# A hybrid attention and DeltaNet layer on one core: two-tensor work off GpSimd in the attention stage, eight buffers for the reloaded attention branch, three DeltaNet tiles in places of their own

## The chip, the core and the metric

The kernel runs on one core of a Trainium2 chip, in one launch. The metric is the device time of that launch in microseconds. Engines are named as in the profile: PE is TensorE, DVE is VectorE, ACT is ScalarE, POOL is GpSimd, and SP issues most of the DMAs. Three runs of the kernel before took 1337.43, 1338.98 and 1342.21 us; the median is 1338.98 us.

## What is computed

One step of a one-layer encoder over 592 tokens (16 meta tokens, 512 of the prompt, 64 of a sample) of width 1024. The parts that matter here:

```
h = RMSNorm(x);  proj = h @ w_in        # columns: q, k, v | DeltaNet q, k, v | z | beta, alpha | gates A, B
A: 8 heads, two 64-wide softmax maps per head, RMS norm of each q and k map (q_norm, k_norm),
   relative bias, block-causal mask, w = p0 - lam * p1, o = w @ v, RMS norm per head
B: 8 heads of 128, causal conv + SiLU, gated delta rule;  o_b = RMSNorm(o_b) * gdn_norm * SiLU(z)
mix = sigmoid(gA) * (o_a @ w_br_a) + sigmoid(gB) * (o_b @ w_br_b);  x = x + mix @ w_out
x = x + relu(RMSNorm(x) @ w_up)^2 @ w_down
```

The outputs are the new rows, and the keys, values and states of both streams.

## The kernel before, in words

Every weight product is taken in three passes of a reduced-precision float type: a matrix is split into a high part (ACT, a cast) and a low part (a subtraction), and high*high, high*low and low*high are summed in PSUM. The weights are streamed in tasks of 256 columns (`stream`, line 300): SP loads two halves of 512 KB, ACT casts them to `wh`, and `lower` (line 348) subtracts to `wl`, on DVE or POOL as `VG` (line 287) decides. `feat` (line 470) runs one task: four groups of 24 matmuls (8 chunks of the contraction, 3 passes each), each group into one of three PSUM banks `pg`.

The order of the whole program is written at build time. `drive` (line 449) lets the weight tasks go forward by 8 matmuls at a time, and between them advances side chains (DeltaNet, attention units, norms) when a model of the engines' times (`Pace`, line 53) says that their inputs are ready. Each engine then runs its own list in that order, and so does each DMA queue. `VG` compares the model's times of DVE and POOL; the model knows no mutual hindrance of the two.

The tasks run in this order: DeltaNet q, k and v, z (SiLU gate), attention q, k, v of the first four heads, gate B, q, k, v of the other four, gate A, branch B (`bb`), branch A (`ba`), w_out, up and down.

- `delta(g)` (line 881), once for each half of the DeltaNet heads: at its end it scales the output, transposes it into `pf`, ACT multiplies it by `gdn_norm`, and SP stores it to `ob_d`. The second half loads its v only after the first half is done.
- `attn_tasks` (line 1199) evacuate q, k, v with an ACT copy and store them to `at_d`. `attend_prep` (line 1233) reloads one head and does three POOL multiplications of 128x640: k and q by their inverse norms `rn`, and k by `k_norm` (`kn_bc`).
- `attend` (line 1291) has 40 units (8 heads of 5 query blocks): scores on PE, bias and maximum on DVE, exponentials on ACT, the combination of the two maps on DVE, transposes on PE, values on PE.
- `load_ob` (line 1418) runs beside them. It reloads the DeltaNet output (`ma`) and z (`mb`), multiplies them on POOL, and waits for `hidden`, which is set when gate A, the last user of the normed input `hh`, `hl`, has issued its matmuls. Then it splits the eight chunks into the memory of `hh` and `hl`, and the branch B tasks start (`br_b_tasks`, line 1437). Three of the four may run beside the attention (HELD, line 47).
- After the attention's memory is released, `load_oa` (line 1481) reloads the attention output through SP in two buffers and splits it for branch A. `residual` (line 1489) loads x again through POOL's queue, one buffer, and transposes it.

The lines that set the places are 589 to 600, 1682 and 1692:

```
ob = [x[:, :, 0:TQ] for x in (hh, hl)]
ab_ = Tags(pace, at_, qk=4, v=3, past=3, sc=SC, mx=6, wT=WT, ob=8, oz=2, ...
mg = Tags(pace, mg_, oa=2, xt=1)
```

Of the kernel before, what the change touches and what calls it, by code (L numbers as in the profile page):

```python
# [8 lines left out]
F32 = mybir.dt.float32  # L9
# [8 lines left out]
P = 128  # L18
# [27 lines left out]
WT = 2  # L46
HELD = 3
MASKED = -32768.0

# [161 lines left out]
def stream_step_kernel(  # L211
# [30 lines left out]
    def bank(name):  # L242
        return pt.tile([P, 512], F32, name=name, tag="pt")
# [36 lines left out]
    def store(dst, src):  # L280
        pace.store(Q, dst, src)
# [5 lines left out]
    def VG(out, n):  # L287

        if "tail" in done:
            return V  # L290
        return V if max(pace.t["DVE"], pace.t["PE"]) + 1.05 * n <= max(pace.t["POOL"], pace.t["PE"]) + out * n else G
# [177 lines left out]

    def feat(xh, xl, nm, evac, m=P, ms=(0, P), halves=QHALVES, after="start", last=None, turn=False):  # L470

        def body(w):
            parts, full = [(h, c) for h in range(len(ms)) for c in (halves[::-1] if turn and h else halves)], deque()
            if "start" not in done:
                parts.sort(key=lambda x: x[1])
            for h, (a, b) in parts:
                while len(full) == PG:
                    yield False
                ps = pg.tile([P, 512], F32, name=f"pg_{nm}{h}{a}", tag="pg")
                n = 0  # L480
                for kc in range(KC):
                    for ww, xx in ((w[0], xh), (w[0], xl), (w[1], xh)):
                        xk = xx[kc] if isinstance(xx, list) else xx[:, kc]
                        TE.matmul(ps[:m, :b - a], ww[:, kc, ms[h]:ms[h] + m], xk[:, a:b], start=n == 0, stop=n == 3 * KC - 1)
                        n += 1
                        if n % QUANTUM == 0 and n < 3 * KC:
                            yield
                full.append((h, ps[:m, :b - a], a, b))
                if last and h == len(ms) - 1 and b == TQ:
                    done.add(last[0])  # L490
                    while last[1] not in done:
                        yield False
                while full and after in done:
                    evac(*full.popleft())
                yield
        return body
# [91 lines left out]
    at_d = [dp.tile([H, P, NT, P], F32, name=f"at_d{i}") for i in range(3)]  # L588
    z_d, oa_d, mb_d = ([dp.tile([P, TQ], F32, name=f"{nm}{j}") for j in range(KC)] for nm in ("z_d", "oa_d", "mb_d"))
    ob_d = dp.tile([H, P, T], F32, name="ob_d")  # L590
# [8 lines left out]
    hq, lq = (x[:, :, N0:T] for x in (hh, hl))  # L599
    ob = [x[:, :, 0:TQ] for x in (hh, hl)]  # L600

# [279 lines left out]
    def delta(g):  # L881
# [251 lines left out]
        V.scalar_tensor_tensor(c1, c1, 0.5, r, ALU.mult, ALU.mult)  # L1133
        yield
        for s in range(NT + 1):
            if s:
                c0, n = TILES[s - 1]
                pf = bank(f"pf{g}{s}").rearrange("p (h i) -> p h i", h=4)
# [4 lines left out]
                store(ob_d[h0:h0 + 4, :, c0:c0 + n].rearrange("h d i -> d h i"), oT[:, :, :n])  # L1143
# [35 lines left out]
    def z_tasks(cs):  # L1179
        out = []  # L1180
        for c in cs:
            def evac(h, ps, a, b, c=c):
# [7 lines left out]
                if b == TQ:  # L1190
                    store(z_d[j], th)
                    done.add(f"z{c}")
            out.append(Task(f"z{c}", w_in[0], OFF_Z + c * 256, feat(hq, lq, f"z{c}", evac)))
# [39 lines left out]
    def attend_prep(hd):  # L1233
# [184 lines left out]
    def load_ob():  # L1418

        while not has("delta0", "delta1", *[f"z{c}" for c in range(4)])():  # L1420
# [12 lines left out]
        for j in range(KC):  # L1433
            split(ob[0][:, j], ob[1][:, j], obs[j])
        done.add("ob")

    def br_b_tasks():
        out = []
        for c in range(4):
# [10 lines left out]
            def body(w, c=c, evac=evac):  # L1450
                yield from feat(ob[0], ob[1], f"bb{c}", evac)(w)
                if c == 3:
                    done.add("br_b")
# [27 lines left out]
    def load_oa():  # L1481
        for j in range(KC):
            a = mg.tile([P, TQ], F32, name=f"oa{j}", tag="oa")
            Q.dma_start(a, oa_d[j])
            yield
            split(late["oh"][j], late["ol"][j], a)
        done.add("oa")

    def residual():

        x1 = late["x1"]
        for t, (c0, n) in enumerate(QTILES):
            xt = mg.tile([P, D], F32, name=f"x_r{t}", tag="xt")
            G.dma_start(xt[:n], x_prompt[0, c0:c0 + n] if t < 4 else x_sample[0])
            yield pace.free(xt) + 4000
            for q in range(2):
# [177 lines left out]
    with pool("delta", side="right") as db_:  # L1674
# [4 lines left out]
        chains.append(Chain(conv_out()))  # L1679
        drive(lambda: not chains and has("delta0", "delta1")())  # L1680
    with pool("attn", side="right") as at_:
        ab_ = Tags(pace, at_, qk=4, v=3, past=3, sc=SC, mx=6, wT=WT, ob=8, oz=2, aoss=3, bias=2, osb=3,
                   aqT0=2, aqT1=2, akT0=2, akT1=2)
# [4 lines left out]
    with pool("mix", side="right") as mp:  # L1688
        for nm in ("mxh", "mxl"):
            late[nm] = [mp.tile([P, TQ], F32R, name=f"{nm}{j}", tag=f"{nm}{j}") for j in range(KC)]  # L1690
        with pool("merge", side="right") as mg_:
            mg = Tags(pace, mg_, oa=2, xt=1)
            for nm in ("oh", "ol"):
                late[nm] = [mg.tile([P, TQ], F32R, name=f"{nm}{j}", tag=f"{nm}{j}") for j in range(KC)]
            done.add("merge")
            chains.append(Chain(load_oa()))
            drive(has("br_b"))
            hp_cm.__exit__(None, None, None)
            xp = ctx.enter_context(pool("x1"))
# [66 lines left out]
```

## Time and profile before

| | us |
|---|---|
| median of three runs | 1338.98 |
| the profiled execution, its own time | 1335.53 |
| its span, first to last instruction | 1333.6 |
| PE busy in the span | 1286.3 |
| DVE, ACT, POOL busy | 855.6, 611.3, 181.4 |

The span is in 25,734 instructions. A row of a group gives engine, operation, what is written from what, the shape and the count, then the busy time and the mean duration of one, then the idle time ahead of it and what ended that. Most rows carry the line of a helper that issues every operation, so they are told apart by the names of tiles. Consecutive matmuls overlap, so the duration of one is more than twice the step from one to the next. The attention's units run from about 584 to 784 us of the span, branch A starts at about 818 us.

### The profile page before, as it was taken

The page shows a single profiled execution, that of the slowest core. Times are in us where ns is not written, and L with a number is a line of the kernel's source. Part 1 is how long each engine was busy: PE and PEld are TensorE (multiplying, and loading weights), DVE is VectorE, ACT ScalarE, POOL GpSimd, SP SyncE. Part 2 cuts the span into 40 slices and gives each one's busy share as a digit, 9 for nine tenths or more (in the row PEclk, how much of TensorE's full clock was granted, in tenths as well). Part 3 has the DMA queues.
Part 4 walks back from the last instruction along what each step waited for, and adds up shares of the span by engine and source line. Part 5 has one row for each costly group of instructions (what it writes and reads, how often), then busy time and mean ns, then how long its engine had stood idle before and what let it go on. Part 6 is the DMA issues. An engine that isn't in the chain of part 4 may idle for free.

```text
span 1333.6 us, 25734 instructions
## 1 busy us (share of the span) xinstructions
PE 1286.3 (96%) x10177; PEld 1242.1 (93%) x10177; DVE 855.6 (64%) x1842; ACT 611.3 (46%) x1438; POOL 181.4 (14%) x251
## 2 busy tenths in 40 slices
PE   7999999999999999999798997999999999999998
PEld 5989999999999999998787886999999999999998
DVE  5766999334377525267777853345678678678687
ACT  5565544333752333366465742224453443453442
POOL 3111513100330000252422102310000000000000
PEclk9999999999999999999899898999999999999999
DMA  6324244423644423774444336542223322323322
GB/s 165 91 67 155 61 145 129 144 81 88 206 118 135 144 60 95 228 235 129 161 131 142 122 124 211 182 141 80 80 80 95 96 80 87 105 62 97 110 76 76
DMA packets 163806, 160.55 MB, mean 120 GB/s; under 512 B 23531, under 2 KB 143613, under 8 KB 163686
## 3 DMA queue, kind: packets, MB, share of 16 engines
q1 hardware_dynamic: 161574, 153.11, 37.7%
q0 software_dynamic: 2112, 5.80, 1.5%
q8 instruction: 80, 1.31, 0.4%
q14 instruction: 40, 0.33, 0.1%
HBM read 123.94 MB, written 37.88 MB: 121 GB/s over the span
## 4 chain that ended last, share of the span: by engine, by line
PE 83%; DVE 6%; DMA 4%; ACT 3%; issue 2%; SPq 0%; POOL 0%; DVEq 0%; ACTq 0%; POOLq 0%
PE pg_u L165 15%; PE pg_a L165 11%; PE pg_d L165 8%; PE pg_g L165 7%; PE pg_ba L165 4%; PE pg_z L165 4%; PE pg_o L165 4%; PE pd_dn L165 4%; PE pa_dn L165 4%; PE pc_dn L165 4%; PE pg_bb L165 3%; PE ppo L165 2%; PE pb_dn L165 2%; DMA bias_d<-bv_d 2%; PE po L165 1%
## 5 line engine op out<-in xcount | busy, mean ns | idle before, releaser
L165 PE MATMUL pg_u<-h2h,wh_u 128*128 128x288 f32 x512 | 151.5, 296 | 0.0
L165 PE MATMUL pg_u<-h2h,wl_u 128*128 128x288 f32 x512 | 151.3, 296 | 0.0
L165 PE MATMUL pg_u<-h2l,wh_u 128*128 128x288 f32 x512 | 151.3, 295 | 0.0
L165 PE MATMUL pg_a<-wh_a,hh 128*128 128x256 f32 (+1 forms) x480 | 136.3, 284 | 1.3 <-ACT sq L165 1.3
L165 PE MATMUL pg_a<-wh_a,hl 128*128 128x256 f32 (+1 forms) x480 | 136.3, 284 | 0.0
L165 PE MATMUL pg_a<-wl_a,hh 128*128 128x256 f32 (+1 forms) x480 | 135.4, 282 | 0.0
L165 PE MATMUL pg_d<-hh,wh_d 128*128 128x336 f32 (+1 forms) x384 | 115.8, 302 | 0.0
L165 PE MATMUL pg_d<-hl,wh_d 128*128 128x336 f32 (+1 forms) x384 | 115.6, 301 | 0.0
L165 PE MATMUL pg_d<-hh,wl_d 128*128 128x336 f32 (+1 forms) x384 | 115.5, 301 | 0.0
L165 PEld LDWEIGHTS pg_u<-h2h,wh_u 128*128 128x128 f32 x512 | 96.1, 188 | 0.1
L165 PEld LDWEIGHTS pg_u<-h2l,wh_u 128*128 128x128 f32 x512 | 96.1, 188 | 0.0
L165 PEld LDWEIGHTS pg_u<-h2h,wl_u 128*128 128x128 f32 x512 | 96.1, 188 | 0.0
L165 PEld LDWEIGHTS pg_a<-wh_a,hh 128*128 128x128 f32 (+1 forms) x480 | 86.5, 180 | 2.4 <-ACT sq L165 1.9
L165 PEld LDWEIGHTS pg_a<-wh_a,hl 128*128 128x128 f32 (+1 forms) x480 | 86.6, 180 | 0.7 <-issue 0.6
L165 PEld LDWEIGHTS pg_a<-wl_a,hh 128*128 128x128 f32 (+1 forms) x480 | 86.5, 180 | 0.4 <-issue 0.2
L165 PE MATMUL pg_g<-hh,wl_g 128*128 128x288 f32 x256 | 78.2, 305 | 0.0
L165 PE MATMUL pg_g<-hh,wh_g 128*128 128x288 f32 x256 | 77.8, 304 | 0.0
L165 PE MATMUL pg_g<-hl,wh_g 128*128 128x288 f32 x256 | 77.7, 303 | 0.0
L165 PEld LDWEIGHTS pg_d<-hh,wl_d 128*128 128x128 f32 x384 | 72.9, 190 | 0.7 <-issue 0.6
L165 PEld LDWEIGHTS pg_d<-hl,wh_d 128*128 128x128 f32 x384 | 72.6, 189 | 1.0 <-issue 0.6
L165 PEld LDWEIGHTS pg_d<-hh,wh_d 128*128 128x128 f32 x384 | 72.7, 189 | 0.2
L165 DVE SCALAR_TENSOR_TENSOR cv_d<-pre_d,vec,cv_d 128x595 f32<-128x595 f32 x72 | 61.6, 861 | 14.7 <-ACT cv_d L165 7.9
(401 smaller groups left out, 3839.0 us busy)
## 6 DMA issues: line engine op xcount, KB each, us to landing
wr_u<-in_w_up_dram SPq DMA_DIRECT2D x32, 512.0 KB, 4.3
wr_dn<-in_w_down_dram SPq DMA_DIRECT2D x32, 512.0 KB, 3.7
wr_d<-in_w_in_dram SPq DMA_DIRECT2D x24, 512.0 KB, 5.1
wr_a<-in_w_in_dram SPq DMA_DIRECT2D x24, 512.0 KB, 3.7
wr_g<-in_w_in_dram SPq DMA_DIRECT2D x16, 512.0 KB, 5.8
at_d<-st SPq DMA_DIRECT2D x48, 128.0 KB, 2.5
th_d<-gt SPq DMA_DIRECT2D x16, 288.0 KB, 2.3
wr_z<-in_w_in_dram SPq DMA_DIRECT2D x8, 512.0 KB
```

Source lines behind the costliest of these rows:

```text
L165: r = f(*a, **kw)
```

## The change

1. `VG` answers DVE for as long as the attention stage is built (from the flag `attn` to the flag `merge`), so the weights' low parts are subtracted on DVE there.
2. The multiplication of k by `k_norm` moves into the evacuation of k (`attn_tasks`): a DVE multiplication out of PSUM takes the place of the ACT copy. The two multiplications by `rn` in `attend_prep` go from POOL to DVE.
3. z is multiplied into the DeltaNet output in `delta`: z is reloaded there in pieces, and one DVE operation out of PSUM with two factors (`gdn_norm` and z) takes the place of the ACT one. The chain first waits until its z is there. `load_ob` loads only the product; its POOL multiplication and the `mb` loads go.
4. Three of the eight chunks of the branch B input get tiles of their own (pool `own`), and are split before `hidden`. The first `bb` task begins the first three of its four groups with these chunks (`lead` in `feat`).
5. `load_oa` gets eight buffers, all loaded at the start of the merge stage through POOL's queue. `x` gets three buffers, two of them loaded there too.

```diff
     def VG(out, n):
-        if "tail" in done:
+        if "tail" in done or "attn" in done and "merge" not in done:
             return V
...
+            begun = {}
+            for h, (a, b) in parts[:PG if lead else 0]:
+                ps = begun[h, a] = pg.tile([P, 512], F32, name=f"pg_{nm}{h}{a}", tag="pg")
+                for kc in range(lead):
+                    for i, (ww, xx) in enumerate(((w[0], xh), (w[0], xl), (w[1], xh))):
+                        TE.matmul(ps[:m, :b - a], ww[:, kc, ms[h]:ms[h] + m], xx[kc][:, a:b], start=kc == i == 0, stop=False)
+                yield
...
+        while not has(*[f"z{h0 + j}" for j in range(4)])():
+            yield
+        zls = {}
         for s in range(NT + 1):
+            if s < NT:
+                c0, n = TILES[s]
+                m0 = max(N0 - c0, 0)
+                zls[s] = a2(f"zl{s}")
+                Q.dma_start(zls[s][:, :, m0:n], z_d[g][:, :, c0 + m0 - N0:c0 + n - N0].rearrange("h d i -> d h i"))
...
-                oT = a2(f"oT{s}")
-                S.activation(oT[:, :, :n], pf[:, :, :n], AF.Copy, scale=gdn_col)
+                oT = zls.pop(s - 1)
+                V.scalar_tensor_tensor(oT[:, :, m0:n], pf[:, :, m0:n], gdn_col, oT[:, :, m0:n], ALU.mult, ALU.mult)
...
-                S.copy(x[:n], ps)
+                if i == 1:
+                    kx, kp = (y.rearrange("t (h d) -> t h d", d=64) for y in (x[:n], ps))
+                    V.tensor_tensor(kx, kp, kn_bc[:n, None, :].to_broadcast([n, 4, 64]), ALU.mult)
+                else:
+                    S.copy(x[:n], ps)
...
-            G.tensor_tensor(xv, xv, rn[:, p, i, :, 2 * h:2 * h + 2, None].to_broadcast([P, NT, 2, 64]), ALU.mult)
-        kv = k.rearrange("p t (m d) -> p (t m) d", d=64)
-        G.tensor_tensor(kv, kv, kn_bc[:, None, :].to_broadcast([P, 10, 64]), ALU.mult)
+            V.tensor_tensor(xv, xv, rn[:, p, i, :, 2 * h:2 * h + 2, None].to_broadcast([P, NT, 2, 64]), ALU.mult)
...
-            b = ab_.tile([P, TQ], F32, name=f"mb{j}", tag="oz")
             Q.dma_start(obs[j], ob_d[j][:, N0:T])
-            Q.dma_start(b, z_d[j])
             yield
-            G.tensor_tensor(obs[j], obs[j], b, ALU.mult)
+        for j in range(OWN):
+            for o in ob:
+                o.append(late["own"].tile([P, TQ], F32R, name=f"own{j}{len(ob[0])}", tag=f"own{j}{len(o)}{o is ob[0]}"))
+            split(ob[0][j], ob[1][j], obs[j])
             yield
         while "hidden" not in done:
             yield
-        for j in range(KC):
-            split(ob[0][:, j], ob[1][:, j], obs[j])
+        for j in range(OWN, KC):
+            for o, x in zip(ob, (hh, hl)):
+                o.append(x[:, j, 0:TQ])
+            split(ob[0][j], ob[1][j], obs[j])
...
         for j in range(KC):
-            a = mg.tile([P, TQ], F32, name=f"oa{j}", tag="oa")
-            Q.dma_start(a, oa_d[j])
-            yield
+            a = late["oa"][j]
+            yield pace.free(a)
             split(late["oh"][j], late["ol"][j], a)
+            yield
...
-            mg = Tags(pace, mg_, oa=2, xt=1)
+            mg = Tags(pace, mg_, oa=8, xt=3)
+            late["oa"] = [mg.tile([P, TQ], F32, name=f"oa{j}", tag="oa") for j in range(KC)]
+            for j in range(KC):
+                G.dma_start(late["oa"][j], oa_d[j])
+            late["xt"] = deque(turn_x(t) for t in range(2))
```

## Rows read from the trace of the kernel before

**Rows 1.** Busy time by stretch: length, PE, PEld, DVE, ACT, POOL, clock, DMA share, GB/s

```profile
584.00:784.00 200.00, 181.42 (x1390) 161.10 (x1387) 154.86 (x511) 123.88 (x378) 49.94 (x79) 0.96 0.45 141
784.00:836.30 52.30, 43.69 (x288) 40.99 (x287) 16.51 (x34) 14.01 (x20) 10.20 (x6) 0.87 0.59 195
836.30:1333.60 497.30, 492.06 (x3702) 490.26 (x3701) 344.04 (x611) 200.06 (x330) 11.98 (x7) 1.00 0.31 97
```

**Rows 2.** Waits of PE: total us, times, longest

```profile
PE pwT L165 <- DVE sc L165: 6.6, 4, 5.0
PE pg_ba L165 <- ACT oh L165: 5.4, 2, 3.5
PE pwT L165 <- DVE mx L165: 4.4, 2, 3.0
PE pg_bb L165 <- ACT hh L165: 2.9, 1, 2.9
PE pg_ba L165 <- DVE ol L165: 2.3, 4, 1.6
PE psc L165 <- DVE mx L165: 1.7, 1, 1.7
```

**Rows 3.** Timeline at 636 to 645 us, one POOL, two DVE and one PE instruction

```profile
635.90 1.42 POOL L165 TENSOR_TENSOR ma<-ma,mb 128x576 f32<-128x576 f32 x1 [6.08 <-DMA mb<-z_d]
...
635.97 1.38 DVE L165 TENSOR_SCALAR aory<-aorv 128x5 int32<-128x5 int32 x1
...
642.66 0.17 DVE L165 SCALAR_TENSOR_TENSOR aort<-aory,aorv 128x5 f32<-128x5 f32 x1
...
644.61 1.33 PE L165 MATMUL pwT<-ident,sc 128*128 128x128 f32 x5 [5.00 <-DVE sc L165]
```

**Rows 4.** POOL's groups by shape from 556 to 784 us

```profile
L165 POOL TENSOR_TENSOR k<-k,kn_bc 128x640 f32<-128x640 f32 x8 | 12.6, 1581 | 0.0
L165 POOL TENSOR_TENSOR ma<-ma,mb 128x576 f32<-128x576 f32 x8 | 11.4, 1423 | 16.6 <-DMA mb<-z_d 16.6
...
L165 POOL TENSOR_TENSOR wl_g<-wr_g,wh_g 128x1024 fp32r<-128x1024 f32 x3 | 7.1, 2374 | 0.0
```

**Rows 5.** DVE's groups by shape from 556 to 784 us

```profile
L165 DVE SCALAR_TENSOR_TENSOR mx<-mx,lam 128x1 f32<-128x1 f32 x32 | 14.3, 445 | 1.1
...
L165 DVE TENSOR_TENSOR wl_g<-wr_g,wh_g 128x1024 fp32r<-128x1024 f32 x5 | 6.1, 1214 | 0.0
...
L165 DVE TENSOR_TENSOR hl<-ma,hh 128x576 fp32r<-128x576 f32 x8 | 5.4, 751 | 1.8 <-ACT hh L165 1.8
```

**Rows 6.** Stretches with the lower clock, columns as in rows 1

```profile
640.00:650.00 10.00, 5.39 (x30) 5.30 (x30) 8.01 (x20) 1.71 (x5) 3.13 (x6) 0.66 0.32 87
685.00:690.00 5.00, 4.78 (x28) 4.30 (x26) 2.21 (x11) 4.05 (x14) 0.00 (x0) 0.66 0.25 88
737.00:745.00 8.00, 7.00 (x31) 6.66 (x32) 7.17 (x10) 7.63 (x15) 1.81 (x1) 0.57 0.46 150
822.00:837.00 15.00, 8.87 (x35) 7.30 (x34) 3.32 (x5) 4.87 (x7) 4.25 (x2) 0.54 0.47 157
```

**Rows 7.** Timeline of ACT where branch B begins

```profile
737.11 4.67 ACT L165 CAST hh<-ma 128x576 fp32r<-128x576 f32 x8
```

**Rows 8.** Tile oa: its loads by SP, first and last start

```profile
L165 SPq DMA_DIRECT2D oa<-oa_d x8: 320/405/1394, 795.1 to 827.8; - x8
```

**Rows 9.** DMA issues from 776 to 842 us: KB each, median us to landing

```profile
oa<-oa_d SPq DMA_DIRECT2D x8, 288.0 KB, 4.1
...
x_r<-in_x_prompt_dram POOLq DMA_DIRECT2D x2, 512.0 KB, 5.5
```

**Rows 10.** Timeline, end of DeltaNet's first half (ACT) and the second half's v (SP)

```profile
353.49 0.68 ACT L165 ACTIVATE oT<-pf,vec 128x512 f32<-128x512 f32 x1
...
367.61 0.43 SPq L165 DMA_DIRECT2D vT<-qkv_d  x1
```

**Rows 11.** PE's groups by shape from 584 to 784 us, one of branch B's three passes

```profile
L165 PE MATMUL pg_bb<-hl,wh_bb 128*128 128x288 f32 x51 | 16.7, 328 | 0.2 <-DVE hl L165 0.2
```

More of the change, by code (lines that the diff above doesn't have):

```diff
@@ L47 @@
 HELD = 3
+OWN = 3
 MASKED = -32768.0
@@ L468, in drive, with feat @@
         pace.flush()
-    def feat(xh, xl, nm, evac, m=P, ms=(0, P), halves=QHALVES, after="start", last=None, turn=False):
+    def feat(xh, xl, nm, evac, m=P, ms=(0, P), halves=QHALVES, after="start", last=None, turn=False, lead=0):
         def body(w):
@@ L478, in body @@
                     yield False
-                ps = pg.tile([P, 512], F32, name=f"pg_{nm}{h}{a}", tag="pg")
-                n = 0
-                for kc in range(KC):
+                ps = begun.pop((h, a), None)
+                k0 = 0 if ps is None else lead
+                if not k0:
+                    ps = pg.tile([P, 512], F32, name=f"pg_{nm}{h}{a}", tag="pg")
+                n = 3 * k0
+                for kc in range(k0, KC):
                     for ww, xx in ((w[0], xh), (w[0], xl), (w[1], xh)):
@@ L588, in stream_step_kernel @@
     at_d = [dp.tile([H, P, NT, P], F32, name=f"at_d{i}") for i in range(3)]
-    z_d, oa_d, mb_d = ([dp.tile([P, TQ], F32, name=f"{nm}{j}") for j in range(KC)] for nm in ("z_d", "oa_d", "mb_d"))
+    oa_d, mb_d = ([dp.tile([P, TQ], F32, name=f"{nm}{j}") for j in range(KC)] for nm in ("oa_d", "mb_d"))
+    z_d = [dp.tile([4, P, TQ], F32, name=f"z_d{g}") for g in range(2)]
     ob_d = dp.tile([H, P, T], F32, name="ob_d")
@@ L599, in stream_step_kernel @@
     hq, lq = (x[:, :, N0:T] for x in (hh, hl))
-    ob = [x[:, :, 0:TQ] for x in (hh, hl)]
+    ob = [[], []]
     def load_x(pl, t):
@@ L1134, in delta @@
         yield
+        while not has(*[f"z{h0 + j}" for j in range(4)])():
+            yield
+        zls = {}
         for s in range(NT + 1):
+            if s < NT:
[3 more added lines that the diff above has]
+                Q.dma_start(zls[s][:, :, m0:n], z_d[g][:, :, c0 + m0 - N0:c0 + n - N0].rearrange("h d i -> d h i"))
             if s:
                 c0, n = TILES[s - 1]
+                m0 = max(N0 - c0, 0)
                 pf = bank(f"pf{g}{s}").rearrange("p (h i) -> p h i", h=4)
@@ L1140, in delta @@
                     TE.transpose(pf[:, h, :n], vtok[s - 1][:n, h], ident[:n, :n])
-                oT = a2(f"oT{s}")
-                S.activation(oT[:, :, :n], pf[:, :, :n], AF.Copy, scale=gdn_col)
-                store(ob_d[h0:h0 + 4, :, c0:c0 + n].rearrange("h d i -> d h i"), oT[:, :, :n])
+                oT = zls.pop(s - 1)
+                V.scalar_tensor_tensor(oT[:, :, m0:n], pf[:, :, m0:n], gdn_col, oT[:, :, m0:n], ALU.mult, ALU.mult)
+                store(ob_d[h0:h0 + 4, :, c0 + m0:c0 + n].rearrange("h d i -> d h i"), oT[:, :, m0:n])
             if s < NT:
@@ L1190, in evac @@
                 if b == TQ:
-                    store(z_d[j], th)
-                    done.add(f"z{c}")
+                    store(z_d[j // 4][j % 4], th)
+                    done.add(f"z{j}")
             out.append(Task(f"z{c}", w_in[0], OFF_Z + c * 256, feat(hq, lq, f"z{c}", evac)))
@@ L1418, in load_ob @@
     def load_ob():
-        while not has("delta0", "delta1", *[f"z{c}" for c in range(4)])():
+        while not has("delta0", "delta1")():
             yield
@@ L1450, in body @@
             def body(w, c=c, evac=evac):
-                yield from feat(ob[0], ob[1], f"bb{c}", evac)(w)
+                yield from feat(ob[0], ob[1], f"bb{c}", evac, lead=OWN if c == 0 else 0)(w)
                 if c == 3:
@@ L1482, in load_oa, with turn_x @@
         for j in range(KC):
-            a = mg.tile([P, TQ], F32, name=f"oa{j}", tag="oa")
-            Q.dma_start(a, oa_d[j])
+            a = late["oa"][j]
+            yield pace.free(a)
+            split(late["oh"][j], late["ol"][j], a)
             yield
-            split(late["oh"][j], late["ol"][j], a)
         done.add("oa")
+    def turn_x(t):
+        c0, n = QTILES[t]
+        xt = mg.tile([P, D], F32, name=f"x_r{t}", tag="xt")
+        G.dma_start(xt[:n], x_prompt[0, c0:c0 + n] if t < 4 else x_sample[0])
+        return xt
     def residual():
@@ L1492, in residual @@
         for t, (c0, n) in enumerate(QTILES):
-            xt = mg.tile([P, D], F32, name=f"x_r{t}", tag="xt")
-            G.dma_start(xt[:n], x_prompt[0, c0:c0 + n] if t < 4 else x_sample[0])
-            yield pace.free(xt) + 4000
+            if t < 3:
+                late["xt"].append(turn_x(t + 2))
+            xt = late["xt"].popleft()
+            yield pace.free(xt)
             for q in range(2):
@@ L1680, in stream_step_kernel @@
         drive(lambda: not chains and has("delta0", "delta1")())
+    own_cm = pool("own")
+    late["own"] = own_cm.__enter__()
     with pool("attn", side="right") as at_:
-        ab_ = Tags(pace, at_, qk=4, v=3, past=3, sc=SC, mx=6, wT=WT, ob=8, oz=2, aoss=3, bias=2, osb=3,
+        ab_ = Tags(pace, at_, qk=4, v=3, past=3, sc=SC, mx=6, wT=WT, ob=8, aoss=3, bias=2, osb=3,
                    aqT0=2, aqT1=2, akT0=2, akT1=2)
@@ L1697, in stream_step_kernel @@
             drive(has("br_b"))
+            own_cm.__exit__(None, None, None)
             hp_cm.__exit__(None, None, None)
```

## The prediction
> **What bounds the kernel now.** I read the stretches first. After 836 us PE is busy for 492.06 of 497.30 us at clock 1.00, with a matmul every 0.133 us (492.06 / 3702): there the change has nothing to win. From 584 to 784 us, the attention, PE is idle for 18.6 us and the mean clock is 0.96; from 784 to 836 us it is idle for 8.6 us at 0.87 [rows 1]. So the question is only who makes PE wait in these 252 us. The list of PE's waits, read next, names three places [rows 2]. In the attention PE waits for DVE's `sc` and `mx`, 6.6 + 4.4 + 1.7 us, and four smaller waits add about 1.9: 14.6 us. Where branch B starts it waits 2.9 us for ACT's split (3.1 with a small DVE wait). Where branch A starts it waits 5.4 us for ACT and 2.3 us for DVE, with a wait of 0.9 us for the reloaded x: 8.6 us.
>
> Third, the lower clock. Each of these waits is followed or surrounded by a stretch at the lower level, 1.2 in place of 2.4 GHz: the granted clock is 0.66, 0.66, 0.57 and 0.54 in stretches of 10, 5, 8 and 15 us [rows 6]. Half-clock time is twice the missing share: 6.8, 3.4, 6.9 and 13.8 us. PE's idle time in them is 4.6, 0.2, 1.0 and 6.1 us; of the first, some 1.8 us lies ahead of the fall. What PE did do there took twice as long, so the loss is half of the rest: about 2.0, 1.6, 3.0 and 3.8 us, 10.4 us in all.
>
> Waits and clock together are 14.6 + 3.1 + 8.6 + 10.4 = 36.7 us. That is the most that this change can return by the three places.
>
> **Why DVE is late in the attention.** The timeline decides it [rows 3]. From 635.90 us POOL runs five two-tensor multiplications in a row. A DVE operation on 128x5 elements that starts at 635.97 takes 1.38 us, the four behind it about as long, as if each had to let one POOL instruction pass; when POOL is through, the same kind takes 0.17 us (642.66). The chain of 1 us took 6.7, and PE waited 5.00 us at its end. The DVE group `mx<-mx,lam` shows how common that is: one element per partition, yet a mean of 445 ns over 32 [rows 5], so up to 32 x (0.445 - 0.17) = 9 us lost in that line alone. Adding up, group by group, what DVE's instructions took above the lower quartile of their group gives 23.7 us between 560 and 790 us. All six attention waits of over 0.7 us that are charged to DVE stand behind such bursts.
>
> **The change, part by part.**
>
> Work put on DVE in the attention. POOL's low parts there are three of gate A and B, and two each of the last attention tasks and of branch B: 7 x 1.214 = 8.5 us. The 16 multiplications by `rn` have 640 columns; between 751 ns at 576 and 1214 ns at 1024 that is 0.82 us, 13.1 us [rows 5]. Together 21.6 us; off POOL go these, the eight by `k_norm` and the eight by z, at 1.4 to 2.4 us each [rows 4]. DVE's sum in the attention therefore stays as it was, about 21.6 in against 23.7 out, near 155 of what were 200 us. What changes is its grain: no operation of 0.2 us turns into one of 1.4, and the longest insertion is 1.2 us. That is under what three units in flight can cover, but DVE will be busy for some 83% of a shorter stage, so some waits come back elsewhere. Between nothing recovered (0) and all (14.6 + 3.6 of the clock = 18.2) I take two thirds, **12 us**, since nearly all of the waits lie behind POOL bursts and DVE gets no lighter.
>
> The Trainium skill (Perfetto Trace Analysis, Optimizing Scalar/DVE Operations) says that where DVE is saturated, moving work to GpSimd may make sense, and adds that the two share a port, so that it might not help. By its first half this part would cost up to the moved 21.6 us. The rows stand nearer to its second half.
>
> Branch B's start. ACT's eight splits begin at 737.11, behind exponentials, and take 4.67 us, 0.58 each [rows 7]. With the lead PE has 27 matmuls (3.6 us) that need none of them. But the third leading group needs the PSUM bank of gate A's last group, whose tanh stands on ACT behind five splits: PE does 18 matmuls, 2.4 us, and then waits for about 5 x 0.58 + 0.5 us of ACT work, with a lower clock still likely. So of 3.1 + 3.0 us I take **2.4 us**, the 18 matmuls; bounds 0 and 6.1.
>
> Branch A's start. SP now loads `oa` from 795.1 to 827.8 us, because two buffers and a queue shared with weights and gates space the eight loads out [rows 8]; PE reaches branch A at 818. With eight buffers all eight can go once the memory and the last head's output are there, at about 797 us, and each lands in some 4 to 6 us [rows 9]; ACT and DVE need 8 x 0.75 = 6 us, beside the last branch B task. That is done by about 808 us, ten before it is needed. All of 8.6 + 3.8 us could go; I leave 2.8 for the crowding of the DMAs (below): **9.6 us**, bounds 0 and 12.4. POOL's queue holds nothing urgent behind these loads: its next work is a low part for branch A, and that had its cast only at 804 us.
>
> DeltaNet. Ten DVE operations of 512 columns, at most 0.75 us by the row of 576 columns, replace ten of ACT. They come at the ends of both halves where DVE has just scaled the output and waits. The z tasks are over long before, so the new wait never holds. But the z pieces are loaded step by step by SP, ahead of later weight loads and stores, and each step of the chain now waits in the build's model for a landing. That may draw the end of a half out by 5 to 10 us. The first half has 14 us in hand before v of the second (353.49 against 367.61) [rows 10]; the second would begin the attention later, which the branch B tasks still cover. Twenty evacuations of k go from ACT to DVE at some 0.4 us each, beside full PE work. I take **2 us lost** for all of this; bounds -1 (fewer DMAs in the attention) and 6.
>
> Sum against the profiled execution's own time: 1335.5 - 12 - 2.4 - 9.6 + 2 = 1313.5 us. That execution lies 3.4 us under the median of the runs shown, so the comparable number is 1317, rounded to **1316**.
>
> **The rivals.**
>
> *DVE becomes the bound of the attention.* For it: DVE's sum does not fall and PE's would. Against it: 77% busy now, with the bursts in it. Then the attention gives nothing: 1335.5 - 2.4 - 9.6 + 2 + 3.4 = 1329 us.
>
> *The reloads crowd the queues.* Ten transfers, 2.3 + 1.0 MB, start at once where the DMAs already move 195 GB/s [rows 1]; at 300 GB/s that is 11 us in which branch B's gates come late and DVE and ACT hold evacuations behind splits. The POOL loads are also the slower ones, 5.5 against 4.1 us [rows 9]. Then branch A's gain is gone: 1326 us. The Trainium skill (SBUF — State Buffer, Who interferes with whom) says that a DMA issued from GpSimd starves while DVE runs in a two-port mode. By that rule loads moved to this queue would land later; no row here isolates it.
>
> *All returns:* 36.7 us, 1302 us.
>
> *The waits are not POOL's* and come back in full with another releaser: 1337 to 1342 us, no change.
>
> *Slower: branch B's tasks run out.* Three of the four tasks may fill PE beside the attention. By 784 us 51 of the 96 matmuls of each pass were used [rows 11]; 45 x 3 x 0.133 = 18 us are left. If DVE's moved 21.6 us all lengthen the attention and DeltaNet's end delays it by 10, it ends 32 us later and PE stands for 14 us at its tail, at the lower clock when it goes on (6 us): 1335.5 + 14 + 6 + 2 - 12 = 1345.5, 1349 us by the median. It decides from a delay of 18 us on.
>
> **How the numbers follow.** Forecast (1308 to 1325) 0.52; all returns 0.08; DVE the bound 0.14; crowded queues 0.08; no change 0.08; slower 0.10. About 0.3%, 4 us, is what a measurement of this kernel can tell from no change. The first four cases are faster by more: 0.82; the fifth is 0.08, the last 0.10. The range leaves out the slower case and the far end of full recovery: 1301 to 1338.
>
> **What would show it.** Right: no DVE instruction on 128x1 or 128x5 elements above 0.3 us in the attention; PE's waits for `sc` and `mx` under 5 us in total; no wait for `oh` or `ol`; the clock at 1.00 from 790 us on; a short wait of branch B for gate A's tanh in place of `hh`. Wrong: the waits of `pwT` as long as before with POOL silent; PE idle ahead of the merge stage for lack of tasks; `thb` or `oa` loads that land late.

## The result, and the profile after

The changed kernel takes 1324.71 us in the median of seven runs (1320.44 to 1329.99); the kernel before, run beside it, 1338.98 us (1335.53 to 1342.21). The ratio is 0.9905, with a 95% interval of 0.9886 to 0.9923. It is faster. The median lies 0.3 us inside the slow end of the forecast's range (1308 to 1325); by the ratio (0.9905 x 1338.98 = 1326.3) it would lie outside. 23 us were forecast (1339 - 1316); it gained 14 us by the medians and 12.7 by the ratio. The profiled execution took 1320.44 us, with a span of 1318.7 us. Where kernels of different chips are compared below, their ratios to the kernel before on the same chip are used, times 1339 us; a gain by these differs from that by the medians by up to 1.6 us. By the intervals, a difference of two such ratios is known to some 3 to 5 us. The traces are each of a single execution.

By stretches (length; PE, PEld, DVE, ACT and POOL busy; clock, DMA share, GB/s), for the changed kernel. They answer to [rows 1]:

```profile
584.00:790.00 206.00, 196.19 (x1529) 175.10 (x1527) 149.36 (x527) 131.50 (x399) 9.95 (x59) 0.98 0.47 149
790.00:818.60 28.60, 21.95 (x141) 20.75 (x141) 7.28 (x21) 10.13 (x19) 9.67 (x12) 0.81 0.80 271
818.60:1318.70 500.10, 494.92 (x3711) 493.47 (x3709) 349.02 (x616) 199.98 (x329) 11.53 (x4) 0.99 0.30 94
```

Up to the point where branch A runs without a stop, PE was idle for 27 us before (18.6 + 8.6) and for 16.5 us now (9.8 + 6.7). POOL's 49.94 us in the attention are 9.95, and DVE's sum is nearly what it was, as forecast. But the stretch ahead of branch A still has a clock of 0.81, and PE is idle there for nearly 7 of 28.6 us.

PE's waits in the changed kernel (total us, times, longest), which answer to [rows 2]:

```profile
PE pxr L166 <- DMA x_r<-in_x_prompt_dram: 4.9, 2, 2.5
PE pwT L166 <- DVE sc L166: 3.6, 1, 3.6
PE pot L166 <- DVE osb L166: 2.5, 1, 2.5
PE pg_bb L166 <- ACT gt L166: 1.8, 1, 1.8
PE psc L166 <- DVE akT L166: 0.8, 1, 0.8
PE pwT L166 <- DVE mx L166: 0.7, 1, 0.7
PE ptk L166 <- DVE mx L166: 0.6, 1, 0.6
PE pot L166 <- DVE mx L166: 0.5, 1, 0.5
```

The old names are mostly gone: the 12.7 us for `sc` and `mx` (6.6 + 4.4 + 1.7) are now 5.4 us (3.6 + 0.7 + 0.6 + 0.5), and no wait for `oh` or `ol` is left. The wait for `gt` is the one forecast in place of that for `hh`. Two are new or longer: the transposes of x wait 4.9 us for their loads (0.9 before), and the last units of the attention wait for DVE, 3.6 us for `sc` and 2.5 us for `osb`.

DVE's groups by shape from 556 to 784 us of the changed kernel (busy us, mean ns), which answer to [rows 5]:

```profile
L166 DVE TENSOR_TENSOR wl_g<-wr_g,wh_g 128x1024 fp32r<-128x1024 f32 x8 | 9.6, 1215 | 0.0
L166 DVE SCALAR_TENSOR_TENSOR mx<-mx,lam 128x1 f32<-128x1 f32 x32 | 7.0, 220 | 1.1
L166 DVE TENSOR_TENSOR k<-k,rn 128x640 f32<-128x640 f32 x8 | 6.5, 818 | 0.0
L166 DVE TENSOR_SCALAR aory<-aorv 128x5 int32<-128x5 int32 x7 | 1.2, 172 | 0.2
```

One element per partition costs 220 ns in place of 445, and the operation that took 1.38 us in [rows 3] takes 0.17 each time. A multiplication by `rn` takes 818 ns, against an estimate of 0.82 us.

### The profile page after: what moved, and what is told of

The parts are those of the page before. It is cut to its first block, busy times and chain, and to the rows that moved or that the text cites. A ratio compares the mean times of both kernels' runs of the same rounds, so it can differ in the third digit from the quotient of the medians.

```text
span 1318.7 us, 25741 instructions
## 1 busy us (share of the span) xinstructions
PE 1281.0 (97%) x10177; PEld 1238.5 (94%) x10177; DVE 860.1 (65%) x1884; ACT 603.7 (46%) x1423; POOL 116.4 (9%) x216
## 4 chain that ended last, share of the span: by engine, by line
PE 82%; DVE 5%; DMA 5%; ACT 4%; issue 3%; SPq 1%; POOL 1%; DVEq 0%; POOLq 0%; ACTq 0%
PE pg_u L166 16%; PE pg_a L166 11%; PE pg_d L166 9%; PE pg_g L166 5%; PE pg_ba L166 4%; PE pg_z L166 4%; PE pg_o L166 4%; PE pd_dn L166 4%; PE pa_dn L166 4%; PE pc_dn L166 4%; PE pg_bb L166 3%; PE ppo L166 2%; PE pb_dn L166 2%; DMA bias_d<-bv_d 2%; PE po L166 1%
## 5 line engine op out<-in xcount | busy, mean ns | idle before, releaser
L166 ACT CAST wh_dn<-wr_dn 128x1024 fp32r<-128x1024 f32 x32 | 33.6, 1050 | 81.4 <-DVE wr_dn L166 41.2
```

The lines of the kernel that those rows point to most:

```text
L166: r = f(*a, **kw)
```

## The experiments

### The parts one by one, and POOL's work put back

**p_dve**: the kernel before with parts 1 and 2 alone; z stays in `load_ob`, multiplied on DVE.

```diff
-        if "tail" in done:
+        if "tail" in done or "attn" in done and "merge" not in done:
...
-            G.tensor_tensor(xv, xv, rn[:, p, i, :, 2 * h:2 * h + 2, None].to_broadcast([P, NT, 2, 64]), ALU.mult)
-        kv = k.rearrange("p t (m d) -> p (t m) d", d=64)
-        G.tensor_tensor(kv, kv, kn_bc[:, None, :].to_broadcast([P, 10, 64]), ALU.mult)
+            V.tensor_tensor(xv, xv, rn[:, p, i, :, 2 * h:2 * h + 2, None].to_broadcast([P, NT, 2, 64]), ALU.mult)
...
-            G.tensor_tensor(obs[j], obs[j], b, ALU.mult)
+            V.tensor_tensor(obs[j], obs[j], b, ALU.mult)
```

> The kernel before, with only the two-tensor work of the attention stage moved from POOL to DVE: the low parts, the multiplications by rn, k_norm in the evacuation of k, and z multiplied on DVE in load_ob (not in delta). Theory (POOL's two-tensor operations hold DVE up): DVE's sum in the attention stays near 155 us, no DVE operation on 128x5 elements there takes over 0.3 us, PE's waits for sc and mx fall from 12.7 us to under 5, and DeltaNet's end does not move (547.9 us); 8 to 14 us faster than before, 1325 to 1331. Rival (DVE becomes the bound of the attention): the waits of pwT and psc stay at 10 us or more with POOL silent, and the time is within 4 us of before.

1321.62 us, ratio 0.9885 (0.9867 to 0.9902): 15.4 us gained, more than was expected. PE's waits in it, from the same view as above:

```profile
PE pg_ba L165 <- ACT oh L165: 6.9, 2, 5.1
PE pg_bb L165 <- ACT hh L165: 3.3, 1, 3.3
PE pwT L165 <- DVE mx L165: 2.3, 1, 2.3
```

Of the attention's waits 2.3 us are left, with DVE given all that POOL had. The first and the last score stand at 585.8 and 759.7 us (583.2 and 769.5 before). One thing was missed: DeltaNet's end moved from 547.9 to 560.4 us although z was not touched. So the place of that end follows the order that the build's model writes, not the z pieces alone. This holds for the whole run: PE's list differs from that of the kernel before from 312 us on, well ahead of the attention. The 15.4 us are therefore the gain of the moved work and of another order together; the run with POOL's work put back, below, keeps the order.

**p_z**: the kernel before with part 3 alone.

```diff
...
-                S.activation(oT[:, :, :n], pf[:, :, :n], AF.Copy, scale=gdn_col)
+                V.scalar_tensor_tensor(oT[:, :, m0:n], pf[:, :, m0:n], gdn_col, oT[:, :, m0:n], ALU.mult, ALU.mult)
...
```

> The kernel before, with only z multiplied in delta (and the mb loads and POOL's eight multiplications by z gone). Theory (the step-by-step loads of z draw DeltaNet's ends out): the last pf evacuation moves from 547.9 to about 557 us, the first scores from 583 to about 590; eight POOL operations of 1.4 us fewer give some of it back: between 3 us faster and 6 us slower. Rival (z costs nothing, its cover holds): the last scores come no later than before (769 us) and the time falls by 3 us or more, by the waits that stood behind ma.

1332.93 us, ratio 0.9949 (0.9927 to 0.9970): 6.8 us gained, with DeltaNet ending at 574.8 us, 27 us later than before. Neither side came as written: the theory had at most 3 us gained, and the rival wanted a last score no later than 769 us, which came at 781.6. In this run the late end was covered by the weight tasks beside it. Where the gain is from is not shown; PE's list is another here too, from 341 us on.

**p_merge**: the kernel before with part 5 alone.

```diff
...
-            mg = Tags(pace, mg_, oa=2, xt=1)
+            mg = Tags(pace, mg_, oa=8, xt=3)
...
+            for j in range(KC):
+                G.dma_start(late["oa"][j], oa_d[j])
...
```

> The kernel before, with only the merge stage's buffers and the loads by POOL's queue (oa 8, x 3). Theory: the waits of branch A for oh and ol (7.7 us) go, but the transposes of x now stand ahead of branch A in PE's list and wait for x's loads, some 2 to 5 us; 5 to 9 us faster. Rival (crowded queues): the waits for oh and ol stay above 5 us or thb is late by more, and the time is within 3 us of before.

1331.27 us, ratio 0.9954 (0.9933 to 0.9976): 6.2 us gained. The waits for `oh` and `ol` are gone, and one of 5.4 us for x has come.

**a_ghost**: the changed kernel with POOL work that nobody needs put back, 12 two-tensor multiplications of 128x256 for each head.

```diff
+        for i in range(12):
+            nc.gpsimd.tensor_tensor(ups, ups, ups, ALU.mult)
```

> The changed kernel with twelve POOL multiplications of 128x256 for each head put back, on a tile that nobody reads any more: no data depends on them, and POOL delays only its own small memsets. Theory: DVE operations beside them take 0.5 to 0.7 us where they took 0.17, DVE's sum in the attention rises by 10 to 25 us, PE's waits come back, and the time rises by 6 to 15 us over the changed kernel (1331 to 1340). Rival (POOL hinders nobody, the gain came from the shorter chains): within 3 us of the changed kernel.

1336.16 us, ratio 0.9991 (0.9978 to 1.0004): 11.5 us of the changed kernel's gain are gone, and nothing waits for these products. The build's model does not see them either: PE, DVE and ACT do the same instructions in the same order as in the changed kernel. None of the three waits for POOL from 584 to 795 us, and SP's queue waits 1.5 us in all for it. The groups from 556 to 784 us show the way that it takes:

```profile
L1277 POOL TENSOR_TENSOR ups<-ups 128x256 f32<-128x256 f32 x96 | 69.8, 727 | 7.2
...
L166 DVE TENSOR_TENSOR q<-q,rn 128x640 f32<-128x640 f32 x8 | 8.2, 1022 | 0.0
L166 DVE SCALAR_TENSOR_TENSOR mx<-mx,lam 128x1 f32<-128x1 f32 x28 | 7.4, 265 | 1.0
L166 DVE SCALAR_TENSOR_TENSOR aort<-aory,aorv 128x5 f32<-128x5 f32 x12 | 3.2, 264 | 0.4
```

DVE's own instructions are longer (818 to 1022 for `q`, 220 to 265, 166 to 264 ns). This settles the main step of the prediction: POOL's two-tensor work delays DVE's, and PE by it. The 11.5 us are the price of this load, 69.8 us of POOL; the load of before was another, 49.94 us from 584 to 784 us [rows 1].

The three parts gained 15.4 + 6.8 + 6.2 = 28.4 us alone, and the whole change, with the tiles of their own added, gained 12.7 by its ratio. Something in the whole costs.

### Where the rest went: pairs of parts, and two repairs

**p_dm**: p_dve with part 5 added (the diff is that of p_merge).

> The kernel before, with the two-tensor work of the attention on DVE and the merge stage's eight oa buffers and POOL-queue loads; z stays in load_ob (multiplied on DVE), no tiles of their own. Theory A (the parts add where they touch different places): the two alone gave 16.5 and 6.9 us, so 1315 to 1317, no wait for oh or ol, a wait of some 5 us for x_r. Theory B (what the merge part saves at branch A comes only from POOL's absence and is already in the DVE part): 1321 to 1323, with branch A beginning as late as in the DVE part alone.

1322.07 us, ratio 0.9869 (0.9842 to 0.9895): 2.1 us better than p_dve, with overlapping intervals. Theory B came nearer. Branch A begins at 816.1 us in place of 804.1: 40 transposes of x now stand ahead of it, and PE waits 3.1 us for a load of x and 3.6 us for DVE's evacuations `thb`.

**p_dz**: p_dve with part 3 added (the diff is that of p_z).

> The kernel before, with the two-tensor work of the attention on DVE and z multiplied in delta. Theory A (z in delta draws out the end of DeltaNet by some 10 us, the attention begins that much later, and the branch B tasks run out before its end, so this eats what the DVE part gained): 1325 to 1330, first score after 589 us, PE alone with the attention for its last 10 to 20 us. Theory B (parts add; z in delta alone gave 5.2 us): 1315 to 1318.

1315.35 us, ratio 0.9820 (0.9794 to 0.9846). Theory A, which was my favourite, falls: z in `delta` and the DVE part add, 8.7 us on top, although the first score comes at 592.5 us.

**a_ztail**: the changed kernel, z pieces loaded one step earlier.

```diff
-            if s < NT:
-                c0, n = TILES[s]
+            for u in range(0 if s == 0 else s + 1, min(s + 2, NT)):
+                c0, n = TILES[u]
...
-                zls[s] = a2(f"zl{s}")
-                Q.dma_start(zls[s][:, :, m0:n], z_d[g][:, :, c0 + m0 - N0:c0 + n - N0].rearrange("h d i -> d h i"))
+                zls[u] = a2(f"zl{u}")
+                nc.sync.dma_start(zls[u][:, :, m0:n], z_d[g][:, :, c0 + m0 - N0:c0 + n - N0].rearrange("h d i -> d h i"))
```

> The changed kernel, with each z piece loaded one step earlier in delta, so that no step of the chain waits in the build's model for a landing. Theory A (the drawn-out end of DeltaNet costs): DeltaNet's second half ends near 548 to 552 us instead of 557.6, the first score comes some 5 to 8 us earlier, and the time is 1316 to 1320. Theory B (the attention's length is set by its own chain and PE has filler beside it, the end of DeltaNet does not matter): 1323 to 1326.

1330.29 us, ratio 0.9932 (0.9909 to 0.9954). Both theories missed: DeltaNet ended at 566.6 us, later and not earlier, and the time was 3.6 us longer, with overlapping intervals. The early loads are issued past the build's model, and PE's list differs from 336 us on; why the end moved that way was not found.

**a_resid**: the changed kernel, the transposes of x only after the splits of `oa`.

```diff
         x1 = late["x1"]
+        while "oa" not in done:
+            yield
```

> The changed kernel, with the residual's loads and transposes of x issued only after the splits of oa. Theory A (the 40 transposes of x ahead of branch A, which wait 2.4 and 2.5 us for x_r, and the ACT copies ahead of the splits hold branch A back): 1318 to 1321, branch A begins near 810 us instead of 818.8, the clock at branch A's start is full sooner. Theory B (branch A waits for the last unit of the attention and for oa's landing whatever comes first): within 2 us of 1324.7, with waits for oh in place of those for x_r.

1327.93 us, ratio 0.9919 (0.9891 to 0.9948), no gain; theory B came nearer, with a wait for `ol` in place of `oh`. Branch A did begin at 810.4 us, and then stood, as the timeline of PE and DVE shows:

```profile
819.46 0.61 PE L166 MATMUL pg_ba<-ol,wh_ba 128*128 128x288 f32 x1 [8.68 <-DVE ol L166]
...
818.19 0.46 DVE L166 SCALAR_TENSOR_TENSOR thb<-thb,pg_bb 128x288 f32<-128x288 f32 x1 [13.44 <-DMA thb<-th_d]
818.65 0.76 DVE L166 TENSOR_TENSOR ol<-oa,oh 128x576 fp32r<-128x576 f32 x1
```

All of `oa` had landed by 806 us, but DVE takes its list in order, and ahead of the low parts stands an evacuation that waits for the gate's load `thb`. So with `oa` early, the next thing late is `thb`, whose last load SP issues only at 809.37 us, behind two weight loads. What these wait for is told in the section on branch A's start, for the changed kernel, where it is the same.

### Which part gives the gain back

**a_nomerge**: the changed kernel without part 5.

```diff
-            mg = Tags(pace, mg_, oa=8, xt=3)
+            mg = Tags(pace, mg_, oa=2, xt=1)
```

(with the loads back in `load_oa` and `residual`)

> The changed kernel with its fifth part undone: oa in two buffers through SP's queue, x in one; work on DVE, z in delta and the three tiles of their own stay. Theory A (the tiles of their own are what gave back some 9 us: with them gate A and branch B run ahead of the attention, the three held tasks are used up before its end and its last units run with nothing beside them): 1322 to 1327, all matmuls of the three held tasks done before 775 us, the attention's last score after 775 us. Theory B (the merge part, its 40 transposes of x ahead of branch A, gave it back): 1314 to 1318.

**a_noown**: the changed kernel without part 4.

```diff
-OWN = 3
+OWN = 0
```

> The changed kernel without the tiles of their own: all eight chunks are split into hh and hl after gate A, no leading groups; the rest of the change stays. Theory A (the tiles of their own gave back some 9 us, the merge part nothing): 1314 to 1318, first branch B matmul near 709 us, the attention's last score near 765 us. Theory B (the merge part gave it back): 1322 to 1327.

a_nomerge takes 1330.44 us, ratio 0.9946 (0.9925 to 0.9967); a_noown 1310.42 us, ratio 0.9809 (0.9788 to 0.9829). With p_dz and the changed kernel this is a square of four:

```
ratio to before        without part 5   with part 5
without part 4             0.9820          0.9809
with part 4                0.9946          0.9905
```

The three tiles of their own (with the leading groups) cost 12.9 us with part 5 (0.0096 x 1339) and 16.9 us without. Part 5 is worth 5.5 us where they are, and 1.5 us, within the intervals, where they are not. With and without part 5, PE's list is the same up to the merge stage.

The traces show where the cost begins. The changed kernel and a_noown run alike, 0.08 us apart, from 600 to 622 us. Then ACT and DVE of the changed kernel have this in their timelines:

```profile
622.38 0.66 ACT L166 CAST own<-ma 128x576 fp32r<-128x576 f32 x1
...
623.07 0.76 DVE L166 TENSOR_TENSOR own<-ma,own 128x576 fp32r<-128x576 f32 x1 [1.42 <-ACT own L166]
...
626.08 0.77 DVE L166 SCALAR_TENSOR_TENSOR sc<-sc,mx 128x528 f32<-128x528 f32 x1
...
630.58 0.76 DVE L166 TENSOR_TENSOR own<-ma,own 128x576 fp32r<-128x576 f32 x1 [1.25 <-ACT own L166]
...
636.29 0.76 DVE L166 TENSOR_TENSOR own<-ma,own 128x576 fp32r<-128x576 f32 x1 [1.39 <-ACT own L166]
```

In a_noown the same combination `sc<-sc,mx` comes 2.1 us earlier:

```profile
623.98 0.77 DVE L166 SCALAR_TENSOR_TENSOR sc<-sc,mx 128x528 f32<-128x528 f32 x1
```

Each of the three splits takes 0.66 us of ACT, and holds DVE for 0.76 us and for a wait of 1.25 to 1.42 us, since its cast is only then done: some 6.3 us of DVE in 15 us. PE does not stop: the build's model has put gate A's matmuls there. PE's lists, the same so far, part at 625.66 us, where the changed kernel has another matmul of gate A and a_noown the transposes of the finished `sc`. The windows by tile show the exchange, first the changed kernel's scores (`psc`), then a_noown's (length, PE busy and matmuls, clock, DMA share, GB/s):

```profile
580.00:622.00 42.00, 7.32 (x72) 1.00 0.63 201
622.00:640.00 18.00, 2.02 (x18) 1.00 0.46 142
```

```profile
580.00:622.00 42.00, 7.29 (x72) 1.00 0.65 201
622.00:640.00 18.00, 3.26 (x36) 1.00 0.49 153
```

72 score matmuls each, then 18 against 36. Gate A's count in the same 18 us is 71 against 56, and its last matmul comes at 696.0 against 703.9 us. So the weight tasks run ahead of the attention. Counted along PE's list, the changed kernel has 40 more weight matmuls than a_noown ahead of the 91st score, 72 ahead of the 154th, 48 ahead of the 199th, and 104 ahead of the 217th. The first rise comes with the splits; the second, at some 720 to 744 us, comes when branch B's tasks run, and the leading groups may have a part in it. The branch B matmuls (`pg_bb`) at the other end, the changed kernel's first:

```profile
697.00:740.00 43.00, 25.70 (x168) 1.00 0.45 148
740.00:770.00 30.00, 16.87 (x102) 0.94 0.51 162
```

```profile
697.00:740.00 43.00, 19.02 (x112) 0.96 0.52 164
740.00:770.00 30.00, 16.45 (x104) 1.00 0.29 96
```

By 770 us the changed kernel has used 270 of the 288 matmuls of the three tasks that may run beside the attention, a_noown 216. The changed kernel's last units then have nothing beside them: the waits of 3.6 and 2.5 us above stand at 783.6 and 791.7 us, the clock falls to its lower level there, and the last output comes at 792.8 us, against 780.8 in a_noown. The tables by stretch of a_noown, for comparison with those of the changed kernel:

```profile
584.00:784.00 200.00, 195.29 (x1541) 176.03 (x1540) 151.13 (x538) 132.27 (x400) 11.58 (x62) 0.99 0.51 161
784.00:807.00 23.00, 18.12 (x132) 17.10 (x130) 7.26 (x12) 9.38 (x17) 7.93 (x8) 0.90 0.80 271
```

PE is idle for 9.6 us up to branch A, against 16.5, and the clock is 0.99 and 0.90 against 0.98 and 0.81. Half-clock time (twice the missing share) is 8.6 against 19 us, of which PE loses about half. 6.9 + 5 us of difference answer to 10.5 us of span (1318.7 against 1308.2), as near as a clock given to 0.01 allows.

### The merge stage

**p_dz8**: p_dz with eight `oa` buffers, loaded where they were, through SP.

```diff
-            mg = Tags(pace, mg_, oa=2, xt=1)
+            mg = Tags(pace, mg_, oa=8, xt=1)
```

> The kernel before with the two-tensor work on DVE and z in delta (1315.35 us), and in the merge stage eight oa buffers in place of two, loaded where they were, through SP's queue; x as before, one buffer, its transposes beside branch A. Theory A (the two buffers space the reloads out and cost the 6.0 us of waits for oh and some of the low clock there): 1308 to 1312, no wait for oh over 1 us. Theory B (the reloads are late because SP's queue and the gates' loads hold them, or DVE's splits stand behind a late gate load): 1313 to 1317.

1310.87 us, ratio 0.9802 (0.9779 to 0.9825), as fast as a_noown, and 2.4 us better than p_dz, with overlapping intervals. Theory A has the time right, but not its sign: a wait of 3.0 us for `oh` and 2.0 us for `ol` are left of 6.7.

**a_xfirst**: a_noown with five x buffers, all loaded ahead of the last two `oa`.

```diff
...
-            mg = Tags(pace, mg_, oa=8, xt=3)
+            mg = Tags(pace, mg_, oa=8, xt=5)
...
             for j in range(KC):
+                if j == 6:
+                    late["xt"] = deque(turn_x(t) for t in range(5))
                 G.dma_start(late["oa"][j], oa_d[j])
...
```

> The changed kernel without the tiles of their own (1310.42 us), with five buffers for x in place of three, all five loads issued on POOL's queue ahead of the last two loads of oa, which wait there for the last heads' stores. Theory A (the waits for x_r, 2.23 and 2.38 us, and part of the low clock at branch A's start come from loads of x that POOL issues late, behind those two, behind two low parts and behind their own buffers): 1303 to 1308, no wait for x_r over 0.5 us, branch A begins at 801 to 803 us instead of 807.1. Theory B (branch A waits for the splits of oa on DVE, which stand behind the gate's late load thb, or the five loads at once make thb and oa land later): 1309 to 1314, with waits for ol or oh in place of those for x_r.

1319.37 us, ratio 0.9876 (0.9855 to 0.9897): 9 us slower than a_noown. The waits for x are gone, and PE stood elsewhere. The timelines of PE, DVE and SP:

```profile
798.79 0.61 PE L166 MATMUL pg_bb<-hh,wh_bb 128*128 128x288 f32 x1 [8.50 <-DVE thb L166]
...
798.28 0.82 DVE L166 SCALAR_TENSOR_TENSOR thb<-thb,pg_bb 128x288 f32<-128x288 f32 x2 [15.85 <-DMA thb<-th_d]
...
781.92 1.22 SPq L166 DMA_DIRECT2D thb<-th_d  x1
```

And its DMA issues of x from 770 to 812 us (KB each, median us to landing):

```profile
x_r<-in_x_prompt_dram POOLq DMA_DIRECT2D x4, 512.0 KB, 11.8
...
x_r<-in_x_sample_dram POOLq DMA_DIRECT2D x1, 256.0 KB, 15.6
```

A gate load of 288 KB, issued at 781.92 us, is there only at 798.28, 16.4 us later. In a_noown the same load took 8.1 us (issued at 778.22, there at 786.35). In the ten us from 780 on the DMAs are busy all the time, at 354 GB/s. The queues from 784 to 792 us (packets, MB, share of the 16 DMA engines) show who had them, POOL's queue first and SP's, which the gate load is on, second:

```profile
q0 software_dynamic: 646, 2.36, 76.2%
q1 hardware_dynamic: 601, 0.75, 26.4%
```

The two moved nearly as many packets, but POOL's queue three times the bytes. The x loads take 11.8 us, against 6.4 in a_noown. PE's wait of 8.5 us is near the 9 us lost, and PE's list is that of a_noown throughout. This is the rival of the crowded queues, seen in full.

## Why the prediction was right, and which of its terms were wrong

**The reading of before** held as an upper bound. 36.7 us were said to be there; the two best versions gain some 26 us by their ratios (a_noown 25.6, p_dz8 26.5).

**DVE is late because of POOL:** right. Of the five signs named, three came: no instruction on 128x1 or 128x5 elements above 0.3 us, no wait for `oh` or `ol`, and the wait for gate A's tanh. The waits for `sc` and `mx`, 5.4 us, just missed the 5 named, and the clock did not come. POOL's work put back costs 11.5 us. The term, 12 us, measured 15.4 alone, with the new order in it, inside its bounds of 0 to 18.2. The rule of the Trainium skill weighed there (Perfetto Trace Analysis, Optimizing Scalar/DVE Operations) is decided for its second half: the moved work did not cost DVE's 21.6 us, and DVE is busy for 149.36 of 206 us, where it was for 154.86 of 200.

**Branch B's start** is the step that failed. The prediction counted the 18 matmuls that PE can do early, 2.4 us gained, and bounded the step at 0. It got the wait for gate A's tanh right in kind (1.8 us, where it worked out 5 x 0.58 + 0.5 = 3.4). But for these 18 matmuls three splits moved from behind gate A into the middle of the attention, and none of the six moved instructions was costed at its new place. There they hold DVE for 6.3 us, and what follows costs 12.9 to 16.9 us. a_noown takes out the tiles and the leading groups together; the two were not tried apart. PE's list differs from the first split on, 75 us ahead of the first leading group, and up to 72 of the 104 weight matmuls that run ahead do so before that group; for the rest it is open.

**The slower rival** had the right mechanism, branch B's tasks running out, with the wrong cause. It was to begin with a delay of 18 us in the attention's end. The end (792.8 against 793.6 us for the last output) was not delayed at all; the tasks were used earlier. The build's model puts the tasks wherever it expects the attention not to be ready, so a delay early in the attention does not show as idle time there, but only at its end, as missing tasks.

**Branch A's start** was sized at 9.6 us, and is worth 6.2 alone, 1.5 to 5.5 beside the other parts. Two sentences failed. "POOL's queue holds nothing urgent behind these loads": the loads of x were behind them, and the transposes of x had moved ahead of branch A; and low parts for branch A were behind both (below). And "beside the last branch B task": the splits did not run there. ACT's casts stood behind copies of x, and DVE's low parts behind `thb`, as these rows of the changed kernel show (ACT, DVE, SP):

```profile
808.60 1.07 ACT L166 COPY x<-pxr 128x512 f32<-128x512 f32 x2 [9.12 <-PE pxr L166]
809.56 0.68 ACT L166 CAST oh<-oa 128x576 fp32r<-128x576 f32 x1
...
813.32 0.46 DVE L166 SCALAR_TENSOR_TENSOR thb<-thb,pg_bb 128x288 f32<-128x288 f32 x1 [11.09 <-DMA thb<-th_d]
813.78 0.76 DVE L166 TENSOR_TENSOR ol<-oa,oh 128x576 fp32r<-128x576 f32 x1
...
790.05 7.33 SPq L166 DMA_DIRECT2D oa_d<-oaT  x2
```

The last row is two stores, the first at 790.05 and the second at 797.05 us. `oaT` has one buffer, so ACT filled it again only when the first store had landed, at 796.13 us. The gate load that DVE waits for until 813.32 us comes later, as these rows of the changed kernel show (POOL, SP):

```profile
802.22 4.77 POOL L166 TENSOR_TENSOR wl_ba<-wr_ba,wh_ba 128x1024 fp32r<-128x1024 f32 x2
...
804.66 2.74 SPq L166 DMA_DIRECT2D wr_ba<-in_w_br_a_dram  x2
807.46 0.50 SPq L166 DMA_DIRECT2D thb<-th_d  x1
```

SP waits 8.6 us in all at the two weight loads for POOL, which must first make the low parts from the weights in the same memory, and the gate load stands behind them in SP's list. POOL, in turn, came to the low parts only at 802.22 us: in its list stood the last load of `oa`, which waited 3.77 us for the second store and went at 800.62, and two loads of x. The casts that the low parts need had been done at 798.9 us. So the loads in POOL's queue held up a gate load in SP's, by some 3.3 us; a run with the low parts on DVE in this stage was not tried. The clock, forecast at 1.00 from 790 us, was 0.81.

**DeltaNet** was put at 2 us lost with bounds of -1 and 6. Its end came 9.7 us later (557.6 against 547.9), within the 5 to 10 forecast, and was covered as forecast; but p_dve ends at 560.4 us without the z pieces, and p_dz at 560.4 with them, so that the pieces are the reason is not shown. The sign of the sum was wrong: part 3 gained 6.8 us alone and 8.7 beside p_dve. Where from is only partly seen. The clock of p_dz is 0.992 against 0.985 in p_dve, which is some 19 us of half-clock time (10 of them in a stretch of DeltaNet, last section), and branch B's wait is 1.7 in place of 3.3 us. PE's lists of the two differ from 338 us on; why the one comes out better is open.

**The sum.** From before to the changed kernel by ratios: 15.4 (DVE) + 8.7 (z) + 1.5 (merge) - 12.9 (tiles) = 12.7 us. The forecast, 12 + 2.4 + 9.6 - 2 = 22 us, is off by +3.4 (DVE), +10.7 (z), -8.1 (merge) and -15.3 (tiles): the total is nearer than its terms, since the errors of both signs cancel in part. That the time fell just inside the range is luck: a gain from z, which was forecast as a loss, paid for most of the loss by the tiles, which was forecast as a gain. DVE as the bound fell: it is busy for 149 of 206 us. Crowded queues had the right price, about 10 us, but only in a_xfirst.

The Trainium skill's rule cited with it (SBUF — State Buffer, Who interferes with whom), that a DMA issued from GpSimd starves while DVE runs in a two-port mode, is not decided by any run here. Through POOL's queue `oa` landed in medians of 3.4 us (changed kernel), 4.2 (p_merge) and 4.9 (a_noown), through SP's in 4.2 (p_dve) and 3.2 (p_dz8), each beside other traffic. And the prediction's "slower ones, 5.5 against 4.1 us" compared loads of 512 KB with loads of 288 KB [rows 9].

## What to carry to other kernels

Work made ready early is not free because its user is far off: look at what stands behind it in each engine's list at the place that it moves to. Where one engine is kept full by independent work, a delay of the dependent chain shows as idle time only where that work ends, so count how much of it is left at fixed times in both kernels, and not only the waits. When all loads of a stage are issued at once, look at the smallest load on any queue that someone needs next, and at what else stands behind them on the engine that issues them. And where the order is written at build time, nearly every edit changes it: a run that keeps the order, as that with POOL's work put back, says most about one cause.

## What was not expected of the hardware

A load of 288 KB took some 16 us beside five loads that another queue had issued one to three us earlier; the same load took 8.1 us without them (a_xfirst against a_noown). And the lower clock also came where PE has no idle time in the profile: in p_dve, at DeltaNet's burst of small matmuls, whose windows by stretch are

```profile
470.00:475.00 5.00, 5.00 (x107) 4.66 (x105) 0.26 (x1) 1.91 (x6) 0.00 (x0) 0.70 0.01 3
475.00:480.00 5.00, 5.00 (x59) 4.94 (x56) 2.27 (x4) 2.30 (x5) 0.00 (x0) 0.50 0.40 121
```

PE is busy for 5.00 of 5.00 us in both, at a clock of 0.70 and 0.50. The changed kernel has the same burst at about 460 us with a clock of 1.00; what decides between the two was not tried.
